# Split weights at a step of 16 bytes within widened tiles, and moving operands at other offsets by stage

## The chip, the cores and the metric

The kernel runs on one core of a Trainium2 chip. The metric is the device time of one execution in microseconds (us), as the median of several executions. Besides these there is one profiled execution, whose trace the text reads. TensorE (PE) does the matmuls; PEld is its weight load; DVE (VectorE), ACT (ScalarE) and POOL (GpSimd) do the elementwise work; SP (SyncE) issues nearly all DMAs.

## The reference

A network of two parts on 256 tokens of width 1024, with 256 more context tokens in the second part. All of it is float32, batch 1.

```python
for layer in range(2):                                  # first part
    x = x + 0.5 * swiglu(rmsnorm(x, norm_ffn1[layer]), gate1, up1, down1)   # hidden width 2816
    x = x + hybrid_mixer(rmsnorm(x, norm_mix[layer]), ...)   # hgrn2, gated delta, rg-lru; w_in, w_out
    x = x + 0.5 * swiglu(rmsnorm(x, norm_ffn2[layer]), gate2, up2, down2)
x = rmsnorm(x, norm_final)
for i in range(2):                                      # second part, x and ctx
    sh1, sc1, g1, sh2, sc2, g2 = split_mod(silu(c) @ w_mod[i] + b_mod[i])   # and for c_ctx
    hx = rmsnorm_2(x, norm1_g[i]) * (1 + sc1) + sh1     # hc from ctx alike
    y, yc = even_mixer(hx, hc, ...) if i == 0 else odd_mixer(hx, hc, ...)
    x = x + g1 * y;  ctx = ctx + cg1 * yc               # ctx in i == 0 alone
    f = peer(tokens, ...)    # 8 heads, top 16 of 16384 experts each; x and ctx tokens if i == 0, else x
    x = x + g2 * f[:256];  ctx = ctx + cg2 * f[256:]
return rmsnorm_2(x, final_g)
```

In `even_mixer` the context's own attention (`plain_ctx_attention` over 8 heads and `diff_attention` over 4) depends on `ctx` and on the modulation alone, not on `x`. Its keys and values are used again by the attention of `x`.

## The kernel before

Activations are kept transposed, channels on partitions and 256 tokens along the free axis, in `xT` and `cT`. A weight matrix comes from memory in blocks of 128 x 2048 floats (`raw`, 1 MB each, issued on SP). To reach float32 accuracy each block of 128 x 1024 is split (`wsplit`, `split`) into two fp32r tiles: ACT casts the block to a high part H, and DVE and POOL subtract H from it for the low part L, each a share of the columns (`share` is POOL's). Activations are split in the same way. Then every product is three matmuls (`mm3`, line L235 of the profile: high by high, high by low, low by high). `proj` makes 256 output channels from one `raw` block: 2 halves x 8 blocks x 3 = 48 matmuls of 256 columns, weights stationary and activations moving. `proj_tok` does it the other way, with the activations stationary and the weights moving, for values. In the experts of `peer_both` the moving operand has 512 columns for a part of the groups (both token sets at once).

The weight tiles `wh`, `wl` lie in the pool `wp` with three buffers each; `roomy` adds an extra pool (`wx`, tiles `wxh`, `wxl`, one buffer each) to the stages that have space. `even_ctx` has weight tiles of its own, `wch` and `wcl` with two buffers each, in its own pool, and one load buffer `rawc`. `gap(n)` allocates n bytes that nothing uses, and `set_off` does so in a pool of its own, so both shift what stands behind them: before, every moving operand of `mm3` begins at 64 (mod 256) bytes of a partition and every weight operand at 128 (in `proj_tok` the other way about, moving 128 and stationary 64).

Pools grow from two sides of SBUF: the left (the constants, `wp`, `wx`, then the pool of the stage) and the right (`modulation`, `even_ctx`, the context's queries). Work of a pool on the right can run beside the stage on the left as long as the bytes don't overlap; where tiles of two stages overlap, the later waits until the earlier is done with them (`reuse_waits="tile"`). A scheduler orders the instructions of each engine with estimated times, out of the order of the program, in so far as data and memory allow.

The program's stages, with the functions that call them, are in `tile_network`:

```python
    ffn(1, 0)
    N.prepare()
    mixer(0, lambda: N.modulation(0, A["wmod"]))
    nc.sync.dma_start(cT, A["ctx"])
    N.even_ctx(cT, A["wie"], A["woe"], kv)
    ffn(2, 0)
    ffn(1, 1)
```

then `mixer(1)`, the context's routing, `ffn(2, 1)`, `even_x`, `peer_both`, `odd_mixer` and `peer`. `ffn` goes through 22 blocks of 128 hidden channels: `proj` for gate and up, tanh and products, then `down` with 24 matmuls. `even_ctx` has 12 input units (`wie`: keys, values and queries of the two attentions) and 4 output units (`woe`), with the softmaxes between them: scores into the one PSUM bank `at` (line L235), their maximum on DVE (`nm`, L963), the exponential with its sum on ACT (`g_p`, L968), the reciprocal and the scaling on DVE, the transposes on PE (L986), a copy on ACT (`g_pt`, L990), and the product with the values. `even_x` does the same for `xT`, with the context's keys too. The names in the rows are those of the tiles, so `wch` is the high part of a weight of `even_ctx` and `hH`, `hL` are the normalised activations.

Of the kernel before, what the change touches and what calls it, by code (L numbers as in the profile page):

```python
# [106 lines left out]
class Net:  # L107
    def __init__(self, ctx, tc):
        self.tc = tc
        self.nc = tc.nc  # L110
        pool = lambda name, **k: ctx.enter_context(tc.tile_pool(name=name, bufs=1, **k))
        self.cst = pool("cst")
        self.wp = pool("wp")
        self.ph = None
        self.ws = ("", self.wp, 2, 3)
        self.xp, self.spare, self.nraw = None, None, 0
        self.al = {}
        self.mod, self.mw = {}, {}
        self.nsplit, self.share, self.pooled, self.ngap = 0, 0, 0, 0

    def constants(self, A, C, P):
        nc = self.nc
# [86 lines left out]
        yield  # L209
        self.ws = was  # L210

    def split(self, src, shape, tag, bufs, pool=None, share=0):

        H = self.t(shape, tag + "h", bufs, F32R, pool)
        L = self.t(shape, tag + "l", bufs, F32R, pool)
        self.nc.scalar.copy(H, src)  # L216
        Hf, n = H.bitcast(F32), shape[-1] - share
        if n:
            self.nc.vector.tensor_tensor(L[..., 0:n], src[..., 0:n], Hf[..., 0:n], OP.subtract)  # L219
        if share:  # L220
            self.nc.gpsimd.tensor_tensor(L[..., n:], src[..., n:], Hf[..., n:], OP.subtract)  # L221
        return H, L

    def wsplit(self, src, shape):

        tag, pool, nraw, nw = self.ws
        was = self.pooled
        self.nsplit += 1
        if self.xp and pool is self.wp and self.nsplit % 4 == 0:
            tag, pool, nw = "x", self.xp, 1  # L230
        self.pooled = max(0, self.pooled - 1)
        return self.split(src, shape, "w" + tag, nw, pool, shape[-1] if was else self.share)

    def mm(self, out, l, r, start=True, stop=True):
        return self.nc.tensor.matmul(out, l, r, start=start, stop=stop)  # L235
# [149 lines left out]
    def proj(self, raw, h, tag="pj", first=False):  # L385


        out = self.bank((128, 2, 256), tag)
        W = []
        for j in range(2):  # L390
            W.append(self.wsplit(raw[:, j * 1024:(j + 1) * 1024], [128, 1024]))
            for k in range(8 * (not first)):
                self.block(out, W, h, j, k)
        for k in range(8 * first):
            for j in range(2):
                self.block(out, W, h, j, k)
        return out
# [5 lines left out]
    def proj_tok(self, raw, h, tag="pj"):  # L403

        out = self.bank((128, 2, 256), tag)
        for u in range(2):
            W = self.wsplit(raw[:, u * 1024:(u + 1) * 1024], [128, 1024])
            for tb in range(2):
                for k in range(4):
                    self.mm3(out[:, tb], [q[:, u * 4 + k, tb * 128:(tb + 1) * 128] for q in h],  # L410
                             [q[:, k * 256:(k + 1) * 256] for q in W],
                             u == 0 and k == 0 and tb == 0, u == 1 and k == 3 and tb == 1)
        return out
# [998 lines left out]
    def experts(self, h, grps, u_d, v_d, gd, f=None, quiet=()):  # L1412
# [12 lines left out]

        def hidden(grp):
            acts[grp] = []
            for b in range(4):
                if b % 2 == 0:
                    raw = self.raw(u_d[grp * 2 + b // 2])  # L1430
# [22 lines left out]

        def down(grp):
            As = gated(grp)
            for half in range(2):
                raw = self.raw(v_d[grp * 2 + half])
                if T == 512:
# [46 lines left out]
    def peer_both(self, l, x, ctx, wq_d, keys_d, u_d, v_d, gd, beside):  # L1505

        first, rest = range(0, NFIRST), range(NFIRST, 32)
        with self.tc.tile_pool(name="eh", bufs=1, reuse_waits="tile") as hp, self.psum("ex", act=2, acc=4):
# [8 lines left out]
                    self.acc = e.value  # L1517

            self.ap_, self.na, self.ph = hp, 4, hp
            self.gap(192)  # L1520
            h = (self.t([128, 8, 512], "pH", 1, F32R), self.t([128, 8, 512], "pL", 1, F32R))
            hx, hc = [[q[:, :, j * 256:(j + 1) * 256] for q in h] for j in range(2)]
            self.gb, self.al = dict(n=6), dict(pj="act")
            self.mnorm(ctx, l, 3, 1, hc)
# [21 lines left out]
    def peer(self, l, x, wq_d, keys_d, u_d, v_d, gd):  # L1546
        with self.tc.tile_pool(name="eh", bufs=1, reuse_waits="tile") as hp, self.psum("ex", act=2, acc=4):
            ps, pb = self.ps, self.pb
            self.ap_, self.na, self.ph = hp, 32, hp
            self.gap(192)  # L1550
            h = self.hl()
            self.route(self.queries(x, l, 0, 2, h, True), wq_d, keys_d, gd, 0)
            self.ps, self.pb, self.al = ps, pb, {}
            self.gap(64, hp)
            with self.roomy(), self.tc.tile_pool(name="ex", bufs=1, reuse_waits="tile") as self.ph:
                self.gap(192)
                self.spare, self.xp = self.xp, None
                gen = self.experts(h, range(32), u_d, v_d, gd, quiet=range(6, 20))
                try:
                    while True:  # L1560
                        next(gen)
                except StopIteration as e:
                    self.residual(x, l, 5, 0, e.value)
# [148 lines left out]
def tile_network(ctx: ExitStack, tc: tile.TileContext, A, out, C, P):  # L1712
# [8 lines left out]
    kv = dram.tile([4, 128, 1024], F32, name="kv")  # L1721
    ffn = lambda i, l, *a: N.ffn(xT, N.p(f"norm_ffn{i}{l}"), A[f"f{i}gu{l}"], A[f"f{i}dn{l}"], *a)
    mixer = lambda l, beside: N.mixer(l, xT, A[f"win{l}"], A[f"ba{l}"], A[f"rgw{l}"], A[f"wout{l}"], beside)
    ffn(1, 0)
    N.prepare()
    mixer(0, lambda: N.modulation(0, A["wmod"]))
    nc.sync.dma_start(cT, A["ctx"])
    N.even_ctx(cT, A["wie"], A["woe"], kv)
    ffn(2, 0)
    ffn(1, 1)  # L1730
    mixer(1, lambda: N.modulation(1, A["wmod"]))
    N.route(N.queries(cT, 0, 1, 2, share=768), A["wq0"], A["keys0"], gd[0], 8, "right")
    ffn(2, 1, 448, 256, 9)
# [43 lines left out]
```

## Time and profile before

| what | value |
|---|---|
| executions | 4326.69 and 4339.61 us, median 4333.15 |
| the profiled execution's own time | 4322.06 us |
| its span in the trace | 4320.2 us |
| mean granted clock of TensorE in it | 0.977 of full speed |
| PE busy | 4131.1 us, 96% of the span |
| PEld, DVE, ACT, POOL busy | 88%, 67%, 45%, 34% |
| DMA | 727.44 MB, mean 168 GB/s |

The profiled execution took 1.9 us more than its span, and 11.1 us less than the median of the executions. Shares are of the span. A busy PE is not one at its peak: the end of a matmul is modelled, so the distance from one start to the next tells its pace, and the width of a window without idle time over its number of matmuls is that distance. A granted clock of 1.00 is 2.4 GHz.

### The profile page before, as it was taken

How to read it: one execution, taken by the hardware profiler on the slowest of the kernel's cores; microseconds unless marked ns; L12 is line 12 of the kernel's file. 1: busy time of each engine (PE TensorE's matmuls, PEld its weight loads, DVE VectorE, ACT ScalarE, POOL GpSimd, SP SyncE). 2: the span in 40 equal slices, each digit the busy share in tenths (PEclk: the TensorE clock that was granted, in tenths of full speed). 3: DMA queues.
4: the chain of work that ended last, by engine and by line, in shares of the span. 5: the costliest groups of instructions: out<-in, count | busy, mean ns of one | idle time of the engine just before them, and what ended most of it. 6: DMA issues, size and time to landing. Idle time of an engine off the chain costs nothing.

```text
span 4320.2 us, 77099 instructions
## 1 busy us (share of the span) xinstructions
PE 4131.1 (96%) x31290; PEld 3789.6 (88%) x31290; DVE 2889.0 (67%) x5463; ACT 1949.7 (45%) x2711; POOL 1449.5 (34%) x1274
## 2 busy tenths in 40 slices
PE   8999999999999889999899999999999999899999
PEld 8998899999789877999688888888899799799999
DVE  6685757559589976999544444444665789775555
ACT  4462555446244554556423232232344646644443
POOL 5541544554263200420222222222255231005554
PEclk9999999999999989999999999999999999999999
DMA  6545654453653452556533333333365145686654
GB/s 215 184 153 209 225 180 152 159 202 128 226 208 128 166 195 73 186 184 227 175 109 117 126 117 117 117 115 120 127 209 180 65 157 194 238 287 211 213 194 147
DMA packets 174996, 727.44 MB, mean 168 GB/s; under 512 B 12080, under 2 KB 87088, under 8 KB 103856
## 3 DMA queue, kind: packets, MB, share of 16 engines
q1 hardware_dynamic: 174640, 722.52, 48.0%
q8 instruction: 245, 4.01, 0.4%
q14 instruction: 111, 0.91, 0.1%
HBM read 668.99 MB, written 53.48 MB: 167 GB/s over the span
## 4 chain that ended last, share of the span: by engine, by line
PE 83%; DVE 11%; DMA 2%; ACT 2%; issue 2%; POOL 1%; SPq 0%; DVEq 0%; ACTq 0%; POOLq 0%
PE acc L235 29%; PE act L235 24%; PE pj L235 20%; PE r L235 3%; PE gd L235 2%; DVE wl L219 2%; PE s L235 1%; PE hg L235 1%; DVE g_o L1401 1%; PE o L235 1%; DVE g_e L1397 1%; ACT wh L216 1%; PE pt L986 1%; DVE wcl L219 1%; PE at L235 1%
## 5 line engine op out<-in xcount | busy, mean ns | idle before, releaser
L221 POOL TENSOR_TENSOR wl<-raw,wh 128x256 fp32r<-128x256 f32 (+3 forms) x432 | 621.7, 1441 | 1458.5 <-ACT wh L216 1419.0
L216 ACT CAST wh<-raw 128x1024 fp32r<-128x1024 f32 x592 | 621.4, 1052 | 753.3 <-PE acc L235 298.2
L219 DVE TENSOR_TENSOR wl<-raw,wh 128x768 fp32r<-128x768 f32 (+3 forms) x584 | 619.3, 1062 | 495.3 <-ACT wh L216 490.5
L235 PE MATMUL acc<-eah,wl 128*128 128x256 f32 (+1 forms) x1824 | 572.0, 315 | 5.3 <-POOL wl L221 4.3
L235 PE MATMUL acc<-eah,wh 128*128 128x256 f32 (+1 forms) x1824 | 561.6, 315 | 15.1 <-ACT eah L216 15.1
L235 PE MATMUL acc<-eal,wh 128*128 128x256 f32 (+1 forms) x1824 | 573.5, 315 | 0.7 <-DVE eal L219 0.7
L235 PE MATMUL pj<-hH,wh 128*128 128x256 f32 x1776 | 503.6, 284 | 17.5 <-ACT wh L216 12.3
L235 PE MATMUL pj<-hL,wh 128*128 128x256 f32 x1776 | 503.6, 284 | 6.3 <-DVE hL L347 4.8
L235 PE MATMUL pj<-hH,wl 128*128 128x256 f32 x1776 | 503.0, 283 | 5.7 <-DVE wl L219 5.7
L235 PEld LDWEIGHTS acc<-eah,wh 128*128 128x128 f32 x1824 | 345.4, 190 | 40.1 <-ACT eah L216 15.2
L235 PE MATMUL act<-pH,wh 128*128 128x512 f32 (+1 forms) x1056 | 362.1, 343 | 13.9 <-ACT wh L216 12.8
L235 PEld LDWEIGHTS acc<-eah,wl 128*128 128x128 f32 x1824 | 344.3, 189 | 30.6 <-POOL wl L221 4.5
L235 PEld LDWEIGHTS acc<-eal,wh 128*128 128x128 f32 x1824 | 345.1, 189 | 26.1 <-DVE eal L219 1.0
L235 PE MATMUL act<-pL,wh 128*128 128x512 f32 (+1 forms) x1056 | 361.7, 343 | 2.4 <-DVE pL L328 2.4
L235 PE MATMUL act<-pH,wl 128*128 128x512 f32 (+1 forms) x1056 | 361.6, 343 | 1.8 <-DVE wl L219 1.8
L221 POOL TENSOR_TENSOR wl<-rawx,wh 128x256 fp32r<-128x256 f32 (+3 forms) x165 | 239.4, 1451 | 366.0 <-ACT wh L216 355.2
L216 ACT CAST wh<-rawx 128x1024 fp32r<-128x1024 f32 x192 | 201.7, 1052 | 347.5 <-PE acc L235 140.0
L235 PEld LDWEIGHTS pj<-hH,wh 128*128 128x128 f32 x1776 | 338.2, 191 | 22.0 <-ACT wh L216 12.3
L219 DVE TENSOR_TENSOR wl<-rawx,wh 128x768 fp32r<-128x768 f32 (+3 forms) x190 | 198.7, 1046 | 228.3 <-ACT wh L216 227.8
L235 PEld LDWEIGHTS pj<-hL,wh 128*128 128x128 f32 x1776 | 339.7, 191 | 10.2 <-DVE hL L347 5.8
L235 PEld LDWEIGHTS pj<-hH,wl 128*128 128x128 f32 x1776 | 338.3, 190 | 7.9 <-DVE wl L219 6.7
L235 PE MATMUL act<-hH,wh 128*128 128x256 f32 x896 | 251.8, 281 | 2.6 <-ACT hH L327 1.9
(555 smaller groups left out, 11201.2 us busy)
## 6 DMA issues: line engine op xcount, KB each, us to landing
raw<-u SPq DMA_DIRECT2D x114, 1024.0 KB, 4.9
raw<-v SPq DMA_DIRECT2D x104, 1024.0 KB, 4.9
eG<-gd SPq DMA_DIRECT2D x49, 1024.0 KB, 8.8
rawm<-wmod SPq DMA_DIRECT2D x96, 512.0 KB, 5.7
gd<-rst SPq DMA_DIRECT2D x24, 2048.0 KB, 7.0
raw<-f1gu SPq DMA_DIRECT2D x42, 1024.0 KB, 4.8
raw<-f2gu SPq DMA_DIRECT2D x42, 1024.0 KB, 4.9
rawx<-v SPq DMA_DIRECT2D x42, 1024.0 KB, 4.9
```

Source lines behind the costliest of these rows:

```text
L216: self.nc.scalar.copy(H, src)
L219: self.nc.vector.tensor_tensor(L[..., 0:n], src[..., 0:n], Hf[..., 0:n], OP.subtract)
L221: self.nc.gpsimd.tensor_tensor(L[..., n:], src[..., n:], Hf[..., n:], OP.subtract)
L235: return self.nc.tensor.matmul(out, l, r, start=start, stop=stop)
L986: nc.tensor.transpose(pt[:, kb % 2, qb * 128:(qb + 1) * 128], P[qb][:, kb * 128:(kb + 1) * 128], self.ident)
L1397: nc.vector.tensor_tensor(e.rearrange("p n c i t -> p (n c) i t"), iota2.unsqueeze(1).to_broadcast([128, 4, 128, 2]), ji[:, n0:n0 + 2].rea ...
L1401: nc.vector.tensor_tensor(o, e[:, :, 0:1].to_broadcast([128, 2, 3, 128, 2]), jg[:, n0:n0 + 2].unsqueeze(3).to_broadcast([128, 2, 3, 128, 2 ...
```

## The change

`split` gets an argument `lead`. For a weight it allocates tiles that are 64 floats (256 bytes) wider than the block, and takes the view from `lead` on, where `lead` is 4 * (`turn` mod 16) floats: 0, 16, 32, up to 240 bytes. `turn` is counted up by each `proj`, each `proj_tok`, and each `hidden` and `down` of the experts. All weights of one such step share the offset. The moving operands are moved by stage: `gap` before the activations of the FFNs is 256, 64 and 128 in place of 192 for three of them, which puts these at 128 (`ffn(1,0)`), 192 (`ffn(2,0)`) and 0 (`ffn(1,1)`), while `ffn(2,1)` stays at 64; in `peer_both` and `peer` the activations `h` are allocated ahead of the gap, which puts them at 128. The mixers, both attentions' projections and the experts' `down` keep 64. The number, the kind and the size of all instructions stay the same.

```diff
-    def split(self, src, shape, tag, bufs, pool=None, share=0):
-
-        H = self.t(shape, tag + "h", bufs, F32R, pool)
-        L = self.t(shape, tag + "l", bufs, F32R, pool)
+    def split(self, src, shape, tag, bufs, pool=None, share=0, lead=None):
+
+        if lead is None:
+            H = self.t(shape, tag + "h", bufs, F32R, pool)
+            L = self.t(shape, tag + "l", bufs, F32R, pool)
+        else:
+            H, L = [self.t([128, shape[1] + 64], tag + i, bufs, F32R, pool)[:, lead:lead + shape[1]] for i in "hl"]
...
-        return self.split(src, shape, "w" + tag, nw, pool, shape[-1] if was else self.share)
+        return self.split(src, shape, "w" + tag, nw, pool, shape[-1] if was else self.share, 4 * (self.turn % 16))
...
         out = self.bank((128, 2, 256), tag)
+        self.turn += 1
...
         def hidden(grp):
             acts[grp] = []
+            self.turn += 1
...
             As = gated(grp)
+            self.turn += 1
...
+            h = (self.t([128, 8, 512], "pH", 1, F32R), self.t([128, 8, 512], "pL", 1, F32R))
             self.gap(192)
-            h = (self.t([128, 8, 512], "pH", 1, F32R), self.t([128, 8, 512], "pL", 1, F32R))
...
+            h = self.hl()
             self.gap(192)
-            h = self.hl()
...
-    ffn(1, 0)
+    ffn(1, 0, 256, 0, NFB, 256)
...
-    ffn(2, 0)
-    ffn(1, 1)
+    ffn(2, 0, 256, 0, NFB, 64)
+    ffn(1, 1, 256, 0, NFB, 128)
```

What this does to the room: the six tiles of `wp` and the two of `wx` take 2,048 bytes more of a partition, the four weight tiles of `even_ctx` 1,024. Before, the pool of an FFN ends at byte 130,624 and that of `even_ctx`, on the right, begins at 131,328. After, the pool of `ffn(2,0)` ends at 132,544 and that of `even_ctx` begins at 130,304, so that the last tiles of the one and the first of the other share 2,240 bytes.

The order of the instructions changes at one place. On SP, behind the loads of the modulation's weights (`wmod`), stand the loads of `ffn(2,0)` (`f2gu`, `f2dn`) and of `even_ctx` (`wie`), and the writes of its keys (`ka`). Before:

```order
L195 DMA raw<-f2gu 128x2048
L195 DMA rawx<-f2dn 128x2048
L195 DMA rawc<-wie 128x2048
L195 DMA raw<-f2gu 128x2048
L195 DMA rawc<-wie 128x2048
L195 DMA raw<-f2gu 128x2048
L195 DMA rawx<-f2dn 128x2048
L195 DMA raw<-f2gu 128x2048
L195 DMA rawc<-wie 128x2048
L195 DMA raw<-f2gu 128x2048
L1081 DMA kv<-ka 128x1024
```

and after:

```order
L195 DMA rawm<-wmod 128x1024
L195 DMA rawc<-wie 128x2048 x3
L1086 DMA kv<-ka 128x1024
L195 DMA rawc<-wie 128x2048 x2
L1086 DMA kv<-va 128x1024
L195 DMA rawc<-wie 128x2048 x4
L1086 DMA kv<-kb 128x1024
L195 DMA rawc<-wie 128x2048 x2
L1086 DMA kv<-vb 128x1024
L195 DMA rawc<-wie 128x2048
L195 DMA rawc<-woe 128x2048 x4
L195 DMA raw<-f2gu 128x2048
```

All loads of `even_ctx`, its output weights `woe` too, now stand ahead of the FFN's loads, but for the first three of `f2gu` and one of `f2dn`, which stand further up. On DVE, in the second half of `even_ctx` (`nm`, `ri` and `g_p` are its softmax; `wl`, `gu`, `tanh` and `ffsl` are the FFN's weights, gate and activations), before:

```order
L963 TENSOR_REDUCE nm<-at 128x1
L1005 TENSOR_SCALAR qz<-pj,ccom 128x256
L974 RECIPROCAL ri<-sm 128x1
L1167 TENSOR_TENSOR ri<-ri,nlam 128x1
L1168 SCALAR_TENSOR_TENSOR g_p<-g_p,ri 128x256
L219 TENSOR_TENSOR wl<-raw,wh 128x768
L373 TENSOR_TENSOR gu<-pj,rstd 128x512
L219 TENSOR_TENSOR wl<-rawx,wh 128x768
L377 SCALAR_TENSOR_TENSOR tanh<-tanh,gu 128x256
L219 TENSOR_TENSOR wxl<-raw,wxh 128x768
L219 TENSOR_TENSOR ffsl<-tanh,ffsh 128x256
L219 TENSOR_TENSOR wl<-raw,wh 128x768
```

and after (the lines are numbered five higher there):

```order
L968 TENSOR_REDUCE nm<-at 128x1
L979 RECIPROCAL ri<-sm 128x1
L1171 TENSOR_SCALAR g_p<-g_p,ri 128x256
L968 TENSOR_REDUCE nm<-at 128x1
L1010 TENSOR_SCALAR qz<-pj,ccom 128x256
L979 RECIPROCAL ri<-sm 128x1
L1172 TENSOR_TENSOR ri<-ri,nlam 128x1
L1173 SCALAR_TENSOR_TENSOR g_p<-g_p,ri 128x256
L968 TENSOR_REDUCE nm<-at 128x1
L979 RECIPROCAL ri<-sm 128x1
L1171 TENSOR_SCALAR g_p<-g_p,ri 128x256
L968 TENSOR_REDUCE nm<-at 128x1
```

The FFN's instructions that stood between the softmax's are gone from there; they follow after the last of `even_ctx`. It is the same on PE, ACT and POOL.

## Rows read from the trace of the kernel before

**Rows 1.** The page: span, busy time by engine, the chain's shares by engine.

```profile
span 4320.2 us, 77099 instructions
...
PE 4131.1 (96%) x31290; PEld 3789.6 (88%) x31290; DVE 2889.0 (67%) x5463; ACT 1949.7 (45%) x2711; POOL 1449.5 (34%) x1274
...
PE 83%; DVE 11%; DMA 2%; ACT 2%; issue 2%; POOL 1%; SPq 0%; DVEq 0%; ACTq 0%; POOLq 0%
```

**Rows 2.** Windows: `ffn(1,0)`; end of `mixer(0)` to end of `ffn(1,1)`; `even_x`.

```profile
core 0: us, PE busy (x) PEld busy (x) DVE busy (x) ACT busy (x) POOL busy (x), PEclk, DMA share, GB/s
12.30:206.00 193.70, 187.27 (x1594) 185.92 (x1594) 120.72 (x176) 89.07 (x120) 117.86 (x94) 0.99 0.53 187
432.00:954.70 522.70, 508.75 (x4247) 496.35 (x4246) 332.71 (x552) 255.10 (x407) 274.39 (x213) 0.99 0.50 177
...
1548.00:1731.00 183.00, 174.54 (x1141) 146.93 (x1142) 114.60 (x226) 83.60 (x158) 13.38 (x7) 0.93 0.36 124
```

**Rows 3.** Timeline of PE (start, duration): modulation's tail, norm, first and last `even_ctx` projection.

```profile
431.96 2.37 PE L235 MATMUL pj<-rawm,sc 128*32 128x256 f32 x40
...
455.23 0.60 PE L933 MATMUL pj<-ccom,mrow 128*128 128x128 f32 x4
...
466.93 0.50 PE L235 MATMUL pj<-ones,g_n 128*128 128x1 f32 x4
...
481.32 0.28 PE L235 MATMUL pj<-hH,wch 128*128 128x256 f32 x1
...
800.25 0.28 PE L235 MATMUL pj<-yH,wcl 128*128 128x256 f32 x1
```

**Rows 4.** Timeline of SP's queue: loads of the units of `even_ctx`.

```profile
516.58 0.33 SPq L195 DMA_DIRECT2D rawc<-wie  x1
...
525.91 9.56 SPq L195 DMA_DIRECT2D rawc<-wie  x2
```

**Rows 5.** Groups by form from 460 to 805 us, and tile `rawc`.

```profile
L221 POOL TENSOR_TENSOR wcl<-rawc,wch 128x384 fp32r<-128x384 f32 x32 | 50.6, 1594 | 56.8 <-ACT wch L216 52.6 <-PE pj L235 4.2
...
L216 ACT CAST wch<-rawc 128x1024 fp32r<-128x1024 f32 x32 | 32.9, 1049 | 39.2 <-DMA rawc<-wie 17.9 <-PE pj L235 15.4 <-DMA rawc<-woe 5.9
...
DMA to landing us min/median/max: 4.7/4.8/6.6
```
**Rows 6.** Timeline of all engines, one half of a softmax of `even_ctx`.

```profile
598.76 0.59 PE L235 MATMUL at<-ka,qz 128*128 128x256 f32 x2
...
599.39 0.42 DVE L963 TENSOR_REDUCE nm<-at 128x1 f32<-128x256 f32 x1 [0.28 <-PE at L235]
...
599.85 0.47 ACT L968 ACTIVATE g_p<-at,nm 128x256 f32<-128x256 f32 x1 [1.73 <-DVE nm L963]
...
600.22 0.19 ACT L968 ACTIVATION_READ_ACCUMULATOR g_p<-at,nm 128x1 f32 x1
...
600.45 0.17 DVE L974 RECIPROCAL ri<-sm 128x1 f32<-128x1 f32 x1 [0.63 <-ACT g_p L968]
...
600.65 0.36 DVE L1138 TENSOR_SCALAR g_p<-g_p,ri 128x256 f32<-128x256 f32 x1
...
603.31 0.49 PE L986 MATMUL at<-ccom,g_p 128*128 128x128 f32 x3
...
603.84 0.59 ACT L990 COPY g_pt<-at 128x512 f32<-128x512 f32 x1 [0.17 <-PE at L986]
```

**Rows 7.** Windows without idle time on PE, columns as in rows 2.

```profile
790.00:900.00 110.00, 110.00 (x936) 110.00 (x935) 60.33 (x78) 48.06 (x62) 63.71 (x50) 1.00 0.49 172
2200.00:3000.00 800.00, 800.00 (x3430) 645.30 (x3430) 369.67 (x429) 228.91 (x285) 201.84 (x143) 1.00 0.36 117
3800.00:4200.00 400.00, 400.00 (x3532) 400.00 (x3531) 238.88 (x288) 192.38 (x221) 180.78 (x120) 1.00 0.65 224
```

**Rows 8.** Timeline of PE in a `proj_tok` of `even_x`: the first and the twelfth.

```profile
1574.80 0.28 PE L235 MATMUL pj<-wh,hL 128*128 128x256 f32 x1
...
1576.10 0.28 PE L235 MATMUL pj<-wl,hH 128*128 128x256 f32 x1
```

More of the change, by code (lines that the diff above doesn't have):

```diff
@@ L118, in __init__ @@
         self.mod, self.mw = {}, {}
-        self.nsplit, self.share, self.pooled, self.ngap = 0, 0, 0, 0
+        self.nsplit, self.share, self.pooled, self.ngap, self.turn = 0, 0, 0, 0, 0
     def constants(self, A, C, P):
@@ L1455, in down @@
             As = gated(grp)
+            self.turn += 1
             for half in range(2):
```

## The prediction

> **What bounds the kernel now.** I read the page's shares and its chain first [rows 1]. TensorE (PE) is busy for 4131.1 of 4320.2 us, and 83% of the chain that ends last is PE's; its longest terms are all the three products of line L235. So two things move the time: how fast one matmul follows another, and how much of the span PE idles, 189 us.
>
> The windows by stage [rows 2] say how that idle time is kept so small. In the stretch 432.0 to 954.7 PE is busy for 508.75 of 522.70 us, although attention over the context (`even_ctx`) runs there from 466.9 to 800.5, with a chain of softmax steps that PE waits for. The sister stage `even_x`, which has the stretch 1548 to 1731 to itself, leaves PE idle for 8.5 of 183 us and at a granted clock of 0.93. `even_ctx` is hidden because its instructions stand among those of `ffn(2,0)` and `ffn(1,1)`: PE's rows at its edges and inside [rows 3], and one softmax half [rows 6], where between the score at 598.76 and the transposes at 603.31 PE works off other projections.
>
> For the pace I read windows in which PE has no gap [rows 7]: 110.00 us for 936 matmuls of 256 columns (117.5 ns), 400.00 us for 3532 (113.3 ns), and 800.00 us for 3430 of 512 columns (233.2 ns). The moving and weight offsets are 64 and 128 in all three, so 113.3 and 117.5 stand at the same offsets. The mean of the two, 115, I take for 256 columns where a stretch's own pace is not read. The one place with other offsets is `proj_tok`, moving 128 and weights 64: from 1574.80 to 1576.10 are 11 steps of 118 ns [rows 8].
>
> **The change, part 1: offsets.** No instruction is added: casts, subtractions, loads and matmuls are the same in number and size, and a view that begins 0 to 240 bytes into its tile costs nothing by itself. What it can change is the pace of about 21,000 matmuls of 256 columns and 4,400 of 512. About 10,200 of the former leave 64 (the four FFNs and the experts' hidden halves) and 2,200 of the latter; the rest keep 64, with weights that now start at any step of 16. Bounds: were all 256-column matmuls to go at 113.3 instead of a mean 115, 21,000 x 1.7 ns = 35 us less; all at 117.8 (the slower pace to a decimal), 21,000 x 2.8 = 59 us more. The nearest row for other offsets is `proj_tok` [rows 8], at the slower pace. I take that for the 10,200 that leave 64: 10,200 x 2.5 ns = 25 us, and nothing for the rest, since nothing in the trace shows the weights' offset at work.
>
> **Part 2: room.** Six weight tiles of the `wp` pool and two of the extra pool grow by 256 bytes each, so everything that stands behind them on the left moves up by 2,048 bytes; four tiles of `even_ctx` on the right grow too, so its pool begins 1,024 bytes lower. Before, the FFN's pool ends at byte 130,624 and `even_ctx`'s begins at 131,328: 704 bytes apart, and both live at once. After, with its gap of 64, the pool of `ffn(2,0)` ends at 132,544 and `even_ctx`'s begins at 130,304. They overlap by 2,240 bytes, in the FFN's split activations and the context's keys. So `ffn(2,0)` cannot run beside `even_ctx`. The order shows it: on every engine the instructions of `even_ctx`, which stood in 77 pieces among those of two FFNs on PE, stand in one piece ahead of `ffn(2,0)`, of which only three gate loads, a down load and some casts come first. The cover of the softmax chain is gone. What remains is `even_ctx`'s own projections, each fed by its one load buffer `rawc`.
>
> What the stage takes alone, from the end of `mixer(0)` at 431.96:
> (a) To the first score. The modulation's tail, 431.96 to 455.8, is 23.8 us [rows 3]; the context's norm, 466.93 to 481.32, some 15; then five units of 2048 columns. Loads of `rawc` come 9.3 us apart where the queue does nothing but wait for the buffer (516.58 and the first of two at 525.91 [rows 4]); the pieces agree: 4.8 us to landing, two casts of 1.05 and a POOL subtraction of 1.6 [rows 5]. A unit's 48 matmuls last 48 x 0.115 = 5.5 us, so loads rule. 5.5 + 4 x 9.3 = 42.7. With 2.5 for the last split: 84 us.
> (b) Neighbourhood attention, eight heads. A head has two halves on one bank: matmul 0.59, maximum 0.42, exponential 0.47 and its sum 0.19 [rows 6], 1.67 each; then reciprocal 0.17, scaling 0.36, transposes 0.6, copy 0.59 [rows 6]; with about ten handovers of 0.1 us, 6.1 us. Eight heads are 49, with four value steps of some 2.5 us 59 bare. Beside them run the loads of seven units, 7 x 9.3 = 65 us, and their matmuls, 20 to 28 in a row between steps, and casts delay the chain: 14 x 1.3 us and some 10. I take 59 + 18 + 10 = 87.
> (c) Differential attention, four heads with two softmaxes a half, 4 x 13.3 = 53 by the same steps. (d) Head norm and `put`, 12. (e) Four output projections, 2 + 3 x 9.3 = 30.
> Sum 266. Then two FFNs alone, each 190 by `ffn(1,0)` (193.70 with its start, 187.27 busy [rows 2]): 380. Together 646, where 522.7 stood: **+123 us**.
> Bounds. Low: `even_ctx` as quick as `even_x` alone, 183 us, behind 29 of modulation: 29 + 183 + 380 - 523 = +69. High: as long as it took among the FFNs, 333.6: +220. I stay at the sum, nearer the low end, because its terms are rows of the same stage.
>
> The profiled execution took 4322.06 us, 11 below the median of 4333.15, so: 4322 + 123 + 25 = 4470, and 11 on the median's scale, **4480 us**, +3.4%. About 2% (87 us, a time of 4420) is what a measurement of this kernel can tell from no change.
>
> **Rivals.**
> 1. *Offsets change nothing; only the order does.* The rows bear it out so far as both paces occur at one pair of offsets [rows 7]; `proj_tok` [rows 8] speaks a little against it. 4322 + 123 + 11 = 4456 us. Chance 0.20.
> The Trainium skill, "SBUF — State Buffer", section "Who interferes with whom", gives PE two independent read ports, one for the moving operand and one for the weight load, and says PE never waits on anyone; by that rule this rival holds. That two paces occur at one pair of offsets, with the weights loaded beside every matmul, is not explained by that section.
> 2. *Offsets hurt.* Weights and moving operand come to share a bank of the memory in some steps, and both matmul sizes lose. No row shows a steady pace above 118. I price it half as far above the slower pace as that is above the quicker, 119.7, and 239.4 for 512 columns: 21,000 x 4.7 + 4,400 x 6.2 = 99 + 27 = 126 us, so 4456 + 126 = 4582. Against it stands that the trace shows nothing of the kind. Chance 0.12.
> 3. *Not slower: the pace pays for the order.* Varied weight offsets hold every matmul at the quicker of the two paces, and 512 columns at twice it, 226.5 instead of 233.2: 21,000 x 1.7 + 4,400 x 6.7 = 35 + 29 = 65 us less. 4456 - 65 = 4391, +1.3%. It decides as soon as the offsets give back 37 us, 1.45 ns for each of 25,400 matmuls; to be faster than before they would have to give 123, 4.8 ns, which no row shows. For it: the quicker pace exists, for 3532 matmuls in a row [rows 7]; against: nothing ties it to an offset. Chance 0.08.
> By the Trainium skill's "TensorE: Matmul & The Clock Gate", section "Back-to-back issue gap", an isolated gap at full clock would be the columns over 2.4 GHz and 2.5 ns, 109.2 and 215.8 ns for the two sizes; no stretch here runs at that pace, and by it the time would be some 4260.
> 4. *The stage runs alone as lightly as `even_x`*, +69, with no loss of pace: 4322 + 69 + 11 = 4402. Speaking for it: half as many keys. Against: one score bank and one load buffer where `even_x` has several. Chance 0.04.
> 5. *The change does not do what it says.* The sizes of the tiles fix the addresses, and by them the offsets are as described; what could fail is only their effect, which is rival 1.
>
> **How the numbers follow.** The forecast has 0.56, rival 1 0.20, rival 2 0.12, rival 3 0.08, rival 4 0.04. The range, 4400 to 4600, reaches down to rival 4 (4402; the forecast with +69 is 4426) and up past rival 2 (4582) and the forecast with +220 (4577). Outside are rival 3, most of it, and whatever joins two ends, +220 with rival 2 above all; together I put them at no more than 2 in 10. Slower by over 2%: the forecast (nearly all), rivals 1 and 2, and none of 3 and 4: 0.86. Within 2%: 3 and 4, less a trifle: 0.12. Faster: 0.02, a pace no row shows.
>
> **What would show it.** In the changed kernel's trace, a stretch of some 240 us between `mixer(0)` and `ffn(2,0)` in which PE runs only `pj<-...wch` and `at` tiles with a busy share well under 0.8, at a lower granted clock, with `rawc` loads 9 to 10 us apart, and then two stretches of 190 us for the FFNs; everything behind it later by about the same amount. Windows without a gap give the pace: about 117.5 ns in the four FFNs and in the last stage, 115 in the projections of the mixers, 233 for 512 columns. A stretch under 190 us for `even_ctx`, or over 300, would make the serial term wrong. A pace under 113 or over 119 ns in any stage would make the offsets' term wrong, and a pace that differs between the FFNs (moving 128, 192, 0, 64) would show that it is the offset that counts.

## The result and the profile after

The changed kernel takes 4532.8 us (median of 4530.94 and 4534.70) against 4333.15 before: 4.6% more, ratio 1.0461 with a 95% interval of 1.0391 to 1.0530. The forecast was 4480, in a range of 4400 to 4600. The profiled execution took 4530.94 us, 208.9 more than that of before.

The page of the changed kernel, to be read against [rows 1]; line 235 is now 238:

```profile
span 4529.2 us, 77137 instructions
...
PE 4254.6 (94%) x31290; PEld 3886.9 (86%) x31290; DVE 2894.4 (64%) x5463; ACT 1950.5 (43%) x2711; POOL 1454.2 (32%) x1274
...
PE 80%; DVE 12%; DMA 3%; ACT 2%; issue 2%; POOL 1%; SPq 0%; DVEq 0%; ACTq 0%; POOLq 0%
```

Two things grew. PE is busy for 123.5 us more with as many matmuls (31,290). Not all of that is the offsets' doing: e1_room (below), with all offsets as before, has 4216.4 us, 85.3 more, of which 51.2 lie between the end of `mixer(0)` and that of `ffn(1,1)`, where its granted clock falls as here. On the chain PE's share falls from 83% to 80%, and that of DVE and the DMAs rises by a point each. And PE idles for 274.6 us of the span instead of 189.1. The windows of the changed kernel, columns as in [rows 2], are `ffn(1,0)`, `even_ctx` with the modulation's tail, `ffn(2,0)`, `ffn(1,1)` and `even_x`:

```profile
12.00:212.60 200.60, 194.20 (x1595) 192.84 (x1595) 120.50 (x174) 88.00 (x120) 117.74 (x94) 0.99 0.52 181
442.50:723.80 281.30, 190.56 (x1060) 149.43 (x1061) 101.50 (x225) 82.49 (x166) 53.58 (x35) 0.72 0.25 90
723.80:925.80 202.00, 193.99 (x1596) 192.89 (x1594) 118.31 (x166) 86.65 (x118) 112.01 (x87) 0.97 0.48 167
925.80:1129.20 203.40, 193.20 (x1594) 192.17 (x1592) 118.09 (x162) 87.64 (x123) 115.59 (x91) 0.97 0.47 165
1729.60:1914.30 184.70, 176.36 (x1143) 148.66 (x1143) 114.67 (x226) 83.64 (x158) 13.34 (x7) 0.94 0.36 123
```

From the end of `mixer(0)` (442.5) to the end of `ffn(1,1)` (1129.2) are 686.7 us, where [rows 2] have 522.7: +164.0. `even_ctx` stands alone, PE busy for 190.56 of 281.30 us at a mean granted clock of 0.72, between its levels of 1.2 and 2.4 GHz. The rest, by the first and last matmul of each stage: `ffn(1,0)` 6.8 longer, `mixer(0)` 3.9, the stretch from `ffn(1,1)` to `even_x` 7.0, `even_x` 1.6, `peer_both` 0, `odd_mixer` 2, `peer` 23.8 (871.3 against 847.5). Together 209. Of the 23.8 one profile can't say how much is the offsets' doing: with the offsets of before, `peer` takes 870.6 us in the profile of e1_room.

What PE waits for in the lonely stage (us in total, times, longest):

```profile
PE at L238 <- ACT g_p L973: 20.1, 17, 1.7
PE at L991 <- ACT g_p L973: 12.4, 9, 2.7
PE pj L238 <- ACT wch L219: 11.1, 7, 2.8
PE pj L238 <- DMA rawm<-wmod: 10.8, 6, 4.9
PE at L238 <- ACT g_pt L995: 4.7, 7, 0.7
PE pj L238 <- DVE rsy L261: 4.6, 1, 4.6
```

The softmax's exponentials (`g_p`) come first, the casts of a unit that has just been loaded (`wch`) and the modulation's loads next. Before, with other projections between these steps, PE idled for 14.0 of the 522.7 us of [rows 2]; here it idles for 90.7 of 281.3.

The pace shows in windows of the changed kernel without a gap; each runs from the first matmul of an FFN step to the 72nd, 71 steps of 256 columns (the last two are of `peer`, 95 steps). Columns are the length, PE busy, PEld busy, granted clock, DMA share, GB/s:

```profile
85.66:94.17 8.51, 8.51 (x73) 8.51 (x72) 1.00 0.69 248
119.60:127.88 8.28, 8.28 (x73) 8.28 (x72) 1.00 0.73 262
145.04:153.55 8.51, 8.51 (x73) 8.51 (x72) 1.00 0.35 114
179.19:187.24 8.05, 8.05 (x74) 8.05 (x72) 1.00 0.34 120
1010.09:1018.60 8.51, 8.51 (x73) 8.51 (x72) 1.00 0.34 116
1044.24:1052.29 8.05, 8.05 (x74) 8.05 (x72) 1.00 0.36 121
4436.26:4447.65 11.39, 11.39 (x98) 11.39 (x96) 1.00 0.55 185
4481.80:4492.56 10.76, 10.76 (x97) 10.76 (x96) 1.00 0.57 185
```

8.51 / 71 is 119.9 ns and 8.05 / 71 is 113.4. The first four rows are of `ffn(1,0)` (moving operand at 128), where the weights stand 144, 208, 0 and 64 bytes behind the moving operand (mod 256); the next two are of `ffn(1,1)` (moving 0), with weights 0 and 64 behind; the last two of `peer`'s `down` (moving 64), again 0 and 64 behind. The pace changes from one step to the next with the weights' offset, and the differences 0 and 64 have the same paces at three different places of the moving operand. DMA traffic goes its own way: 0.69 and 0.35 of it at 119.9 ns.

### The profile page after: what moved, and what is told of

Its sections match the earlier page's. It is cut to its first block, busy times and chain, and to the rows that moved or that the text cites. A ratio compares the mean times of both kernels' runs of the same rounds, so it can differ in the third digit from the quotient of the medians.

```text
span 4529.2 us, 77137 instructions
## 1 busy us (share of the span) xinstructions
PE 4254.6 (94%) x31290; PEld 3886.9 (86%) x31290; DVE 2894.4 (64%) x5463; ACT 1950.5 (43%) x2711; POOL 1454.2 (32%) x1274
## 4 chain that ended last, share of the span: by engine, by line
PE 80%; DVE 12%; DMA 3%; ACT 2%; issue 2%; POOL 1%; SPq 0%; DVEq 0%; ACTq 0%; POOLq 0%
PE acc L238 28%; PE act L238 22%; PE pj L238 20%; PE r L238 2%; PE gd L238 2%; DVE wl L222 2%; PE s L238 1%; DMA rawm<-wmod 1%; PE at L238 1%; DVE g_o L1406 1%; DVE wcl L222 1%; PE hg L238 1%; DVE g_e L1402 1%; PE o L238 1%; DMA rawc<-wie 1%
## 5 line engine op out<-in xcount | busy, mean ns | idle before, releaser
L224 POOL TENSOR_TENSOR wl<-raw,wh 128x256 fp32r<-128x256 f32 (+3 forms) x432 | 623.4, 1444 | 1467.1 <-ACT wh L219 1438.9
L238 PE MATMUL act<-pH,wh 128*128 128x512 f32 (+1 forms) x1056 | 362.1, 343 | 15.3 <-ACT wh L219 12.8
```

## The experiments

**e1_room: the order alone.** The kernel before with a larger gap ahead of two FFNs, a multiple of 256 bytes, so that only the room changes:

```diff
-    ffn(2, 0)
-    ffn(1, 1)
+    ffn(2, 0, 256, 0, NFB, 192 + 3072)
+    ffn(1, 1, 256, 0, NFB, 192 + 3072)
```

> The kernel before with 3,072 bytes more ahead of the activations of ffn(2,0) and ffn(1,1): their pool overlaps that of even_ctx, and all offsets (mod 256) stay 64 and 128. Theory (two separate costs, the order by room some 150 us, the pace some 59 us): even_ctx stands alone for some 280 us, the two FFNs behind it take 190 each, and the time is 4333 + 145 = about 4480, between 4465 and 4495. Rival (the offsets make the stage slow, the room alone is harmless because the scheduler only places the stage elsewhere): within 1% of before, 4290 to 4380. Second rival (the granted clock falls in the lonely stage and the FFNs behind it suffer for long): over 4510.

Measured: 4483.1 us, ratio 1.0355 (1.0335 to 1.0374), +152.9 on the 4330.2 of before in the same runs, as the theory had it. Its windows, the lonely stage and the two FFNs:

```profile
435.90:715.00 279.10, 187.47 (x1061) 146.03 (x1060) 101.33 (x225) 82.48 (x166) 53.46 (x35) 0.72 0.25 91
715.00:909.30 194.30, 186.07 (x1595) 185.01 (x1594) 118.37 (x165) 87.98 (x119) 111.21 (x87) 0.97 0.49 174
909.20:1105.80 196.60, 186.38 (x1596) 185.34 (x1594) 117.89 (x162) 89.13 (x123) 114.64 (x91) 0.97 0.49 171
```

279.1 for `even_ctx`, as in the changed kernel, and 194.3 and 196.6 for the FFNs: 669.9 where 522.7 stood, with all offsets those of before. So the overlap of the pools is enough to make the order, and the order makes three quarters of the loss.

**e2_offsets: the offsets alone.** The changed kernel with the room given back:

```diff
-            self.gb = dict(n=4)                    # ffn
+            self.gb = dict(n=nsq)                  # 2 for ffn(2,0), ffn(1,1)
...
-            self.gb = dict(n=3, p=3, pt=4)         # even_ctx
+            self.gb = dict(n=2, p=3, pt=4)
```

> The changed kernel with the offsets kept and the room given back: two buffers instead of four for the squares of ffn(2,0) and ffn(1,1), two instead of three for those of the context's norm, so that the pools no longer overlap and even_ctx stands among the FFNs again. Theory: the order's cost goes, the pace's stays, 4333 + 59 = 4392, between 4380 and 4410; the FFNs at 118 to 120 ns a matmul as in the changed kernel. Rival (offsets cost nothing by themselves, the stages are longer because of what the order did to them): 4333, under 4350. Second rival (the two costs are not additive, the stage stays slow for another reason): over 4450.

Measured: 4378.6 us, ratio 1.0110 (1.0092 to 1.0129), +48.4, a little under the expected range; both rivals fall. `even_ctx` stands among the FFNs again, from 486 to 820 us. 152.9 and 48.4 add up to 201.3, and the change itself cost 199.7. But e2 also has fewer buffers, which cost 14 us by themselves (e10, below). Without these the two parts are 187, and the 12 that are then missing stay unexplained; the interval of the change itself is some 30 us to either side.

**e3_map and e4_fine: the pace by itself.** TensorE alone, on operands that are long in place:

```diff
+    def stretch(m, w, cols, blocks):
...
+                lh, ll = [q[:, w + k * 128:w + k * 128 + 128] for q in W]
+                rh, rl = [q[:, m + k % nb * cols:m + k % nb * cols + cols] for q in M]
...
+    for d in range(0, 64, 2):          # floats; e4: range(1, 64, 2)
+        for rep in range(3):
+            stretch(0, d, 256, 4)
```

> TensorE alone: the fp32r products of the kernel in stretches of 96 (256 columns) or 48 (512 columns), every operand long in place, with the weights' offset minus the moving operand's going through 0 to 248 bytes in steps of 8, three stretches each, and a few other pairs with the same differences; everything else of the network is left out and the output is the input. Theory (the pace goes by the difference alone, mod 256, and no other engine is needed for it): 120 ns at 0, 16, 128 and 144 bytes, 117 at 208 and 224, 113.4 or 118 at 64 and 192; 227 ns for 512 columns at 0, 233 at 64; the same differences give the same pace whatever the moving operand's own offset. Rival (it goes by the weights' own offset or by the moving operand's): pairs with one difference differ by 3 ns or more. Second rival (the difference in pace comes from the other engines' writes to the same memory): one pace within 1 ns everywhere.

> As the first map, TensorE alone, at the differences that it left out: 4, 12, 20 up to 252 bytes, three stretches of 256 columns and one of 512 each; then 512 columns at 0, 120, 240 and 192 again, three times. All else is left out and the output is the input. Theory (the pace goes by the difference, finely and without an order that one could guess): values between 113.3 and 122 ns and 226.7 and 234 ns, most differences with one value, a few with two; 512 columns at 0 and 120 stay at 226.7 each time. Rival (only steps of 16 bytes or more count): each value is that of the nearest multiple of 16 within 1 ns. A difference that holds 113.3 in all three stretches would be a better place than 64.

Windows of e3_map, each from the start of a stretch's 9th matmul to that of its 89th, 80 steps of 256 columns (columns as in [rows 2]): difference 0; 8; 64 twice; then 0 and 64 with the moving operand, and the weights with it, 128 bytes further on; and three of 512 columns, 32 steps, at 0, 64 and 120:

```profile
43.42:53.02 9.60, 9.60 (x82) 9.60 (x81) 0.00 (x0) 0.00 (x0) 0.00 (x0) 1.00 0.01 2
67.39:76.64 9.25, 9.25 (x83) 9.25 (x81) 0.00 (x0) 0.00 (x0) 0.00 (x0) 1.00 0.01 2
320.74:329.81 9.07, 9.07 (x82) 9.07 (x81) 0.00 (x0) 0.00 (x0) 0.00 (x0) 1.00 0.00 0
332.44:341.87 9.43, 9.43 (x83) 9.43 (x82) 0.00 (x0) 0.00 (x0) 0.00 (x0) 1.00 0.01 2
1626.54:1636.14 9.60, 9.60 (x82) 9.60 (x81) 0.00 (x0) 0.00 (x0) 0.00 (x0) 1.00 0.01 2
1638.61:1647.67 9.06, 9.06 (x82) 9.06 (x81) 0.00 (x0) 0.00 (x0) 0.00 (x0) 1.00 0.01 2
1176.75:1184.00 7.25, 7.25 (x33) 6.01 (x32) 0.00 (x0) 0.00 (x0) 0.00 (x0) 1.00 0.00 0
1271.52:1278.99 7.47, 7.47 (x33) 6.02 (x32) 0.00 (x0) 0.00 (x0) 0.00 (x0) 1.00 0.00 0
1354.63:1361.88 7.25, 7.25 (x33) 6.01 (x32) 0.00 (x0) 0.00 (x0) 0.00 (x0) 1.00 0.00 0
```

And of e4_fine, differences 52, 76 and 108:

```profile
235.55:244.62 9.07, 9.07 (x83) 9.07 (x82) 0.00 (x0) 0.00 (x0) 0.00 (x0) 1.00 0.01 2
342.97:352.04 9.07, 9.07 (x82) 9.07 (x81) 0.00 (x0) 0.00 (x0) 0.00 (x0) 1.00 0.01 2
487.22:496.82 9.60, 9.60 (x82) 9.60 (x81) 0.00 (x0) 0.00 (x0) 0.00 (x0) 1.00 0.01 2
```

With DVE, ACT and POOL at 0.00 the same paces appear: 9.60 / 80 is 120.0 ns, 9.25 / 80 is 115.6, 9.07 / 80 is 113.4, 9.43 / 80 is 117.9; 7.25 / 32 is 226.6 and 7.47 / 32 is 233.4. So no other engine is needed, and of e3's two rivals neither holds. Of the theory's values those at 16 and 128 missed: 118.3 ns in place of 120 at 16, and at 128 stretches of both 118.7 and 120.0. At 64 the stretches take one of two paces: of twelve, seven 113.33 and five 117.78, and nothing in between. At 192 it was two and ten. In e4 the values are finer than steps of 16: 113.33 in all three stretches at 52 and 76, 118.3 at 68, 119.4 at 60, so its rival falls. Among the 64 differences, the first stretch of each run left out, 256 columns lie between 113.3 and 123.3 ns and 512 columns between 226.7 and 236.8, a little further up than expected; 0, 120, 132 and 156 have 226.7 for 512. The map's paces are found again in the whole kernel: of the 22 steps of `ffn(1,0)` in the changed kernel, which go through all sixteen differences, the last 19 each have a pace, over 71 steps, within 0.2 ns of one that the map has at the same difference.

**e5_moving: the moving operands alone.** The kernel before with the change's gaps and the order of `gap` and `h`, no wider tiles (`peer` is changed like `peer_both`, which is shown).

```diff
+    ffn(1, 0, 256, 0, NFB, 256)
+    ffn(2, 0, 256, 0, NFB, 64)
+    ffn(1, 1, 256, 0, NFB, 128)
...
+            h = (self.t([128, 8, 512], "pH", 1, F32R), self.t([128, 8, 512], "pL", 1, F32R))
             self.gap(192)
-            h = (self.t([128, 8, 512], "pH", 1, F32R), self.t([128, 8, 512], "pL", 1, F32R))
```

> The kernel before with the moving operands alone put at the change's places (ffn(1,0) 128, ffn(2,0) 192, ffn(1,1) 0, the experts' hidden halves 128); weights stay at 128 and tiles at their width, so room and order are those of before. Theory (difference, by the map's values): ffn(1,0) and peer's hidden halves at difference 0 go at 120 ns, ffn(2,0) at 117, ffn(1,1) at 119 to 120, but the hidden halves of 512 columns at difference 0 fall to 226.7; 31 us by count, so 4333 + 25 to 31, about 4360, between 4345 and 4370, peer_both quicker than before by some 8 us and peer slower by some 18. Rival (a moving operand away from 64 costs 2.5 ns whatever the weights' offset): peer_both not quicker, ffn(1,0) by 4 us longer, not 8. Second rival (no effect): 4333.

Measured: 4356.3 us, ratio 1.0052 (1.0028 to 1.0076), +24.3. `ffn(1,0)` takes 203.6 us (+9.9) and `peer` 864.3 (+16.8), but `peer_both` 1582.5, 8.4 less than before. In the window 2200 to 3000 us of e5, the 512 columns of [rows 7]:

```profile
2200.00:3000.00 800.00, 800.00 (x3476) 650.89 (x3475) 375.25 (x435) 233.25 (x291) 205.21 (x145) 1.00 0.37 119
```

3476 instead of 3430: half of them, at difference 0, gained. That is in the theory's range, and a rule by which leaving 64 costs would not give the gain.

**e6_follow: places moved, difference kept.**

```diff
-        return self.split(src, shape, "w" + tag, nw, pool, shape[-1] if was else self.share, 4 * (self.turn % 16))
+        return self.split(src, shape, "w" + tag, nw, pool, shape[-1] if was else self.share, self.lead)
...
+            was, self.lead = self.lead, (off + 64) % 256 // 4      # ffn
...
+                    self.lead = 16 if h else 0                     # queries; hidden: 16, down: 0
```

> The changed kernel with the room given back, the moving operands at their new places, and every weight tile's offset made to follow: 64 bytes behind the moving operand in each stage, in place of the step of 16. No operand of the four FFNs but one, and none of the experts' hidden halves, stands where it stood before, but the difference is that of before everywhere. Theory (difference alone): as before, 4333, between 4320 and 4345, mean pace 115 and 233.3 ns. Rival (the places themselves count, moving operands away from 64 or weights away from 128): over 4355.

Measured: 4348.8 us, ratio 1.0033 (1.0012 to 1.0054): +16.8, a little over the range. The cut buffers alone have as much (e10, below), so what moved places cost at a kept difference is about nothing (some 3 us, within the noise). It is the difference that counts.

**e7_load2: what the lonely stage is made of.**

```diff
-                self.psum("evenc", "right", pj=1, at=1), self.weights("c", self.ph, 1, 2):
+                self.psum("evenc", "right", pj=1, at=1), self.weights("c", self.ph, 2, 2):
```

> The kernel of the run e1_room (offsets of before, even_ctx alone by lack of room) with two load buffers for even_ctx instead of one. Theory (in the lonely stage the loads of 9.3 us a unit rule the five units ahead of the first score and the output projections, the softmax chain the middle): the five units take 28 us instead of 43, the output projections 22 instead of 30, the middle some 5 less, so 4483 - 28 = 4455, between 4440 and 4468. Rival (the softmax chain and the granted clock rule everywhere): 4483 within 8. Second rival (all of the stage is loads): below 4430.

Measured: 4471.2 us, ratio 1.0318 (1.0296 to 1.0340): 12 less than e1_room, between theory and rival. In its profile the stage itself is 20.8 shorter than the 279.1 of e1_room:

```profile
436.60:694.90 258.30, 180.31 (x1062) 141.60 (x1062) 96.77 (x225) 83.31 (x166) 55.39 (x35) 0.73 0.27 98
```

The first score comes 73.8 us after `mixer(0)` (510.4) instead of 82.2 (518.1), and the neighbourhood part, from there to 596.1, takes 85.7 instead of 96.3. So the loads were worth 8.4 us ahead of the first score, where the step (a) gave them 15, and 10.6 in the middle, where it gave them 5; the differential part (614.4 to about 670 in e1, 596.1 to 651.7 here) didn't change. The end with the output projections, from the head norm's last matmul on, came down by 2 (684.7 to 714.8 in e1, 666.2 to 694.6 here), where the expectation had 8. Between the medians the gain is smaller than in the profile; single executions of these kernels differ by 25 us and more.

**e8, e9, e10, e11: the map put to use.** All moving operands at 64 as before, and one lead for each kind of product:

```diff
-        self.nsplit, self.share, self.pooled, self.ngap = 0, 0, 0, 0
+        self.nsplit, self.share, self.pooled, self.ngap, self.lead = 0, 0, 0, 0, 3
...
+                self.lead = 48 if T == 512 else 3
```

The lines are those of e8: a lead of 3 floats is difference 76, and 48 is difference 0 for 512 columns. e9 and e11 have 61 and 14 there (52 and 120), e10 has 0 (64). The room is given back as in e2; e11 leaves `even_ctx` its tiles and buffers of before, and cuts the FFNs' two alone.

> The kernel before with the widened tiles and the room given back (two buffers for the squares in ffn(2,0) and ffn(1,1), two for the context's), all moving operands at 64, and the weights put by the maps: difference 76 for 256 columns (113.33 ns in all three stretches of the map), 0 for 512 columns (226.67). Theory (the map holds in the full kernel): 21,000 x 1.7 + 4,400 x 6.7 = 35 + 29 = 64 us less, of which some four fifths show, as with the offsets of the changed kernel (48 of 62): 4331 - 50 = about 4280, between 4265 and 4300. Rival (the starts of stretches in the full kernel, with all engines at work, bring other paces than the map's): only the 512 columns gain, 4305 or more. Second rival (starts that are not multiples of 16 bytes make the casts and subtractions slower): over 4330, with longer casts in the groups.

> The same with difference 52 for 256 columns and 120 for 512, the map's other places at 113.33 and 226.67 ns. Theory: as at 76 and 0, 4265 to 4300, and within 10 us of that run. Rival (what holds in the map is chance of its starts): one of the two is slower than the other by over 15 us.

> The same tiles and buffer cuts with every lead at 0, so that the difference is 64 for 256 and 512 columns alike and all operands stand where they stood before: only the wider tiles and the fewer buffers remain. Theory (tiles and buffers cost nothing when the pools don't overlap): 4331 within 10. Rival (the cut buffers cost time, so that the runs with the room given back understate the gain of offsets): 4345 or more.

> The kernel of e9_best52 with less given up for the room: even_ctx keeps its own weight tiles and buffers of before (difference 64 there), only the squares of ffn(2,0) and ffn(1,1) are cut to two buffers, and proj_tok goes to difference 64, since 52 went at 118.9 ns there. Theory (the cuts cost some 14 us in the run e10_cuts, and a part of them was that of the context's norm): 4286 less 0 to 12, 4272 to 4290. Rival (the cuts that cost are those of the FFNs): 4286 within 5. Either way quicker than before by about 1%.

| run | median us | ratio to before, 95% |
|---|---|---|
| e8_best76 | 4305.8 | 0.9942 (0.9916 to 0.9968) |
| e9_best52 | 4285.8 | 0.9895 (0.9864 to 0.9926) |
| e10_cuts | 4342.9 | 1.0038 (1.0013 to 1.0062) |
| e11_best52 | 4275.0 | 0.9871 (0.9849 to 0.9893) |

e11 beats both kernels, that of before by 1.3% and, median against median, the changed one by 5.7%. Its windows at places like those of [rows 7]:

```profile
790.00:900.00 110.00, 110.00 (x973) 110.00 (x972) 61.47 (x78) 48.99 (x64) 62.28 (x53) 1.00 0.51 179
2200.00:3000.00 800.00, 800.00 (x3531) 662.40 (x3531) 370.83 (x442) 237.96 (x297) 193.41 (x148) 1.00 0.37 121
```

973 matmuls in 110 us where 936 stood, and 3531 in 800 where 3430 stood. e11 came out as expected. Its profile is 45.5 us shorter than that of before, and 40.0 of these are PE's busy time:

```profile
PE 4091.1 (96%) x31290; PEld 3775.4 (88%) x31290; DVE 2835.9 (66%) x5463; ACT 1950.7 (46%) x2711; POOL 1365.0 (32%) x1274
```

e8 missed its range and is 20 us slower than e9, as the rival in e9's expectation had it, though in windows at these two places it shows the same pace (973 and 3531 too). In another place it does not. The same matmuls near the end of `peer_both`, in e8 and in e9, and the busy times of both:

```profile
3150.00:3290.00 140.00, 140.00 (x1169) 140.00 (x1168) 74.93 (x85) 63.53 (x73) 72.89 (x49) 1.00 0.56 189
3127.70:3260.10 132.40, 132.40 (x1169) 132.40 (x1168) 72.71 (x85) 63.79 (x73) 68.32 (x49) 1.00 0.59 200
...
PE 4107.5 (95%) x31290; PEld 3789.0 (88%) x31290; DVE 2892.4 (67%) x5463; ACT 1948.8 (45%) x2711; POOL 1447.1 (34%) x1274
PE 4094.7 (96%) x31290; PEld 3778.3 (88%) x31290; DVE 2839.5 (66%) x5463; ACT 1950.9 (46%) x2711; POOL 1353.5 (32%) x1274
```

At difference 76, which had 113.33 ns in all three stretches of the map, e8 goes at 119.8 for 140 us; the same takes e9 132.4 us, 113.3 ns each, at 52. So three stretches do not show that a place holds its pace. Of the 34.2 us between these two profiles 12.8 are PE's busy time; the rest is idle time of PE (202.9 against 181.5 us), and POOL is busier in e8 too (last section). What of this makes the 20 us of the medians is open.

The cuts of e10 cost 14 us by the medians, 6 to 27 by the interval, more than the theory had and a little less than the rival; e2, e6, e8 and e9 carry them, e11 a part.

## Why the prediction was right, point by point

*The sign and the cause.* Shown by e1 and e2: the pools' overlap put `even_ctx` by itself, that costs 153 us, and the offsets cost the rest. Rival 1 (offsets change nothing) fell to e2, rival 2 (both sizes lose, 239.4 ns for 512 columns) to `peer_both`, which took as long as before, rival 3 (the pace pays) to the changed kernel's windows, rival 4 (as light as `even_x`) to the 281 us of the lonely stage.

*The serial term, +123, was too small: 150.* The stage: 281.3 against 266 (a 81.3 against 84; b, from the first score at 523.8 to the first of the differential part at 619.7, 95.9 against 87; c to e together 104 against 95). The FFNs alone: 194.3 and 196.6 in e1 against 190 each. [rows 2] had 193.70 for `ffn(1,0)`; taking 3.7 off "for its start" was the mistake, since an FFN that stands alone has a start of its own, with PE idle and part of it at a lower granted clock. That holds for `ffn(1,1)` too, which follows another FFN. The starts of both in e1:

```profile
715.00:738.30 23.30, 17.27 (x125) 16.60 (x125) 18.08 (x41) 7.26 (x12) 6.48 (x6) 0.85 0.27 91
909.20:932.90 23.70, 16.53 (x121) 15.89 (x120) 18.82 (x41) 10.73 (x21) 7.31 (x7) 0.86 0.37 134
```

In (b) the loads were taken to run beside the chain, with 10 us for what delays it. But e7, which differs from e1 by the second load buffer alone, brings this part from 96.3 to 85.7 us, close to the 87, so the loads are enough to account for the 9 us. In e1 five loads stand behind one another there, 9.2 us apart, from 562.2 to 599.0 us; in e7 they are 7.2 apart, from 551.8 to 580.3. Loads did not rule the first units as strictly as (a) had it: with two buffers (e7) they came down by 8 us, not 15. In (c) to (e) the differential part took 58 us in place of 53 and the output projections 34 in place of 30; why is open.

*The pace term, +25, was too small and rested on the wrong step.* "Nothing for the rest, since nothing in the trace shows the weights' offset at work" failed: `peer`'s `down`, moving at 64 throughout, goes at 119.9 ns where the weights' step comes to difference 0. So did the term for "the 10,200 that leave 64": the place of the moving operand by itself does nothing (e6), and half of the 512 columns became quicker (e5). What counts is the weights' offset minus the moving operand's, mod 256. By the prediction's own sign, a pace over 119 ns, its offsets' term is wrong; that e5 measured +24.3 for the moving operands alone, so near the 25, is chance, since it is a sum of other losses and a gain in `peer_both`. By the maps' means over the sixteen differences, 118.3 ns against the 115 of before and 232.0 against 233.3, the change's offsets are 21,000 x 3.3 - 4,400 x 1.3 = some 63 us more for PE; of these 50 show (4532.8 less the 4483.1 of e1), or 36 if e10 is taken from e2. The [rows 8] value, 118 at difference 192, was one of the differences (192: mostly 117.8), and most of the sixteen lie above it. That views at other offsets cost the other engines nothing held for the sixteen taken together (POOL's subtraction 1444 ns on average, before 1441), but not for each place (last section). Both terms were too small, and the 53 us between forecast and result are the two together. The serial term was right by its mechanism; that the pace term has the right sign is in part luck, since the step it was worked out from does not hold.

The rows that misled were [rows 7]: two paces at one pair of offsets looked like proof that offsets don't matter. The map shows both paces at difference 64 again, with nothing else at work. e1_room shows what that does to one execution. In the same stage as the third of [rows 7], offsets unchanged, its profile has

```profile
3965.00:4365.00 400.00, 400.00 (x3399) 400.00 (x3398) 228.90 (x278) 184.09 (x213) 173.22 (x115) 1.00 0.63 216
```

3399 in place of 3532 (117.7 ns in place of 113.3), and that execution took 4505 us, 22 above its kernel's median. A median over several executions is needed before 1% is read from such a kernel.

*The Trainium skill.* "SBUF — State Buffer", section "Who interferes with whom", says PE's ports for the moving operand and for the weight load are independent and PE never waits on anyone. The map speaks against the independence: with the other engines at 0.00, the pace goes from 113.3 to 120 ns by the two operands' relative place alone. The measurement decides; what in the chip makes it so, no run here shows. "TensorE: Matmul & The Clock Gate", section "Back-to-back issue gap", gives the isolated gap at full clock as the columns over 2.4 GHz and 2.5 ns, by estimate 109.2 and 215.8 ns; no stretch of the maps came below 113.3 and 226.7.

## What to carry to other kernels

A change of tile sizes is a change of the schedule: before its own effect is costed, add up the pools that live at the same time, and see in the built order whether two stages that ran among each other still do; in e1 an overlap of 2,368 bytes (3,072 less the 704 that were free) cost 153 us. Where a stage with dependent steps is hidden among another's matmuls, add up what it takes alone, chain and loads, and the neighbours' full time with their starts: here 281 and 194 and 197 us where 523 stood. Where PE has no gap, count matmuls per window: a pace that differs at one code is worth a map of its own. Other places of the weights gave 1.3% for a few bytes, most of it in PE's busy time. And try a place in the whole kernel before it is believed, as 76 shows.

## What the runs showed of the hardware that was not expected

- For fp32r matmuls, each with its own weight load, the time from one start to the next depends on (weights' offset - moving operand's offset) mod 256, in steps as fine as 4 bytes: 113.3 to 123.3 ns for 256 columns and 226.7 to 236.8 for 512, with no other engine busy (e3, e4).
- At some differences (64, 88, 168 and 192 among them) a stretch of 96 matmuls settles on one of two paces and keeps it: 113.33 or 117.78 ns at 64. Which one, the length of the pause ahead of it did not tell: both came behind the same pause.
- The best place for 256 columns (52 or 76) is not that for 512 (0, 120, 132, 156). The places that were best in the maps don't hold their pace everywhere: of the gap-free runs of 48 matmuls of 256 columns, 34 of 278 go at 120 ns in e8 (76) and 8 of 279 in e11 (52).
- With the weights at 116 (mod 256), and at 184 for 512 columns, POOL's share of the subtraction is some 7% quicker at the same shape. With the weights at 128 (before, e10), or at 140 and 64 (e8), it is not. In e10, e8 and e11:

```profile
L224 POOL TENSOR_TENSOR wl<-raw,wh 128x256 fp32r<-128x256 f32 x358 | 509.5, 1425 | 1192.2 <-ACT wh L219 1166.0 <-DVE wcl L222 13.3 <-DVE rii L1378 3.8
L224 POOL TENSOR_TENSOR wl<-raw,wh 128x256 fp32r<-128x256 f32 x358 | 510.9, 1429 | 1167.4 <-ACT wh L219 1141.8 <-DVE wcl L222 12.7 <-PE pj L238 5.7
L224 POOL TENSOR_TENSOR wl<-raw,wh 128x256 fp32r<-128x256 f32 x358 | 474.8, 1328 | 1192.3 <-ACT wh L219 1165.4 <-DVE wcl L222 13.9 <-DVE req L1379 3.7
```
